# Block sums behind low parts, a late product ahead of a turn, and a filler after each lone dilated score

## The chip, the cores and the metric

The kernel runs on one core of a Trainium2 chip. The metric is the device time of one execution in microseconds (us); the time of a kernel is the median of its runs.

## The reference

A decoder trunk of two layers on 1024 tokens of width 1024, in float32. Each layer normalises its input, makes one wide projection of it, runs two kinds of attention on the parts, gates and merges them, and ends with a convolutional feed-forward network of inner width 2816:

```python
for l in range(DEPTH):                       # DEPTH = 2
    h = rmsnorm(x, norm1[l])
    proj = h @ w_in[l]
    qa, ka, va, qb, kb, vb, gate_pre = jnp.split(proj, splits, axis=-1)
    o_a = dilated_mixture(...)               # windows 128, 512, 2048 at dilations 1, 4, 16; softmax with a slope
    o_b = stick_breaking_attention(...)      # sigmoid(z) times the running product of 1 - sigmoid(z)
    gates = jax.nn.sigmoid(gate_pre + b_gate[l])
    merged = g_a * (o_a @ w_br[l, :OUT_A]) + g_b * (o_b @ w_br[l, OUT_A:])
    x = x + merged @ w_o[l]
    h2 = rmsnorm(x, norm2[l])
    up = h2 @ w_up[l]
    x = x + (gelu(conv(up[:, :D_FF])) * up[:, D_FF:]) @ w_down[l]
return rmsnorm(x, norm_f)
```

## The kernel before

**Products in two parts.** Every float32 operand is split into a high part and a low part (`split`, L130: a cast on ScalarE, L131, and the rest by a subtraction on VectorE, L132), and every product is three matmuls on TensorE: high by high, high by low, low by high. Names with `hi` or `h` at the end (w_hi, t_hi, hh, p0h) are high parts, those with `lo` or `l` (w_lo, t_lo, hl, p0l) are low parts. A weight piece comes by DMA into w_raw or in_a, and ScalarE and VectorE make w_hi and w_lo of it.

**Attention with dense work between.** In the first half of each layer TensorE's order is written by hand. `attend` (L325) goes through 36 items: 16 of stick-breaking attention (B00 to B17), 4 near ones of the dilated mixture with dilation 1 (N00 to N11), and 16 far ones (T00 to T17). An item has scores (L603, L604: z from keys and queries), turns (transposes of the probabilities: L659 for B, L730 for N, L834 to L836 for T) and products of the turned probabilities with the values (L670 for B, L742 for N, L844 and L846 for T). A turn is followed by `parts` (L606), which makes the high and low part of the turned probabilities. The product of one turn comes after the next turn, and the last product of an item, `late`, is carried over into the next item, where it stands behind the first turn. Between all these steps stands dense work, the projections: `dense.advance(rate)` adds the rate of the phase to a sum and emits one step, six matmuls of 128x512, whenever the sum passes 1. It also calls `aside`, which emits one step of side work. `dense.step()` emits a step of dense work alone. The dense steps up to N11 are plain products (L168 to L170); after it come the seven-products (L918 to L920).

**Seven-products and block sums.** The gates, far keys, queries and values are multiplied as two-by-two blocks with seven block products in place of eight. For this, sums of the blocks of the normalised input are needed: S[3], S[1], S[2] and S[4], each of four pieces of 128x512. `block_sums` (L924) plans them as side work: S[3] after B14 and B17, S[1] from the scores of N01 on, S[2] from those of N11 on, S[4] after that. A step `first` (L941 to L943) makes a piece of a sum by three operations on GpSimd, `further` (L950, L951) makes a later sum from the one before by two on VectorE, all in the tile h_sum, and `in_two` splits a piece into t_hi and t_lo (S[4] into the places of hh and hl). The products of a pair (`pair_rest`, `run`) take S[2] first (into the bank i_a, which L1064 then adds to u), then S[1] (into i_c, L1069), then S[3] (into i_a again, L1077), h itself, and S[4]. Ahead of them GpSimd makes sums of the weight blocks in four operations (L1044, L1047, L1050, L1051).

**Who orders what.** TensorE takes its instructions as they are written. On VectorE, ScalarE, GpSimd and the DMA queue of SyncE a scheduler sets the order when the program is built; `tc.high_priority` raises some instructions, among them those of `parts`, and `tc.issue_after(x)` keeps instructions behind x in the order of their engine.

Of the kernel before, what the change touches and what calls it, by code (L numbers as in the profile page):

```python
# [11 lines left out]
ALU = mybir.AluOpType  # L12
# [4 lines left out]
T = 1024  # L17
# [30 lines left out]
def f32(ap):  # L48
    return ap.bitcast(F32)
# [3 lines left out]
def trunk_kernel(ctx, tc, x, norm1, w_in, b_gate, w_br, w_o, norm2, w_up, conv_w, conv_b, w_down, norm_f, out, depth=None, probe=None):  # L53
# [75 lines left out]

    def split(hi, lo, src, eng=None):  # L130
        act.copy(hi, src)  # L131
        (eng or dve).tensor_tensor(lo, src, f32(hi), ALU.subtract)  # L132


    def weights(src, cols, place=None):
# [189 lines left out]
    def attend(dense, items):  # L325

        late = None
        for i, (name, first, rest, rate, make) in enumerate(items):  # L330
            if i == 0:
                dense.until(first)
                dense.step()
                dense.step()
                sc, micro = make()
                for f in sc:
                    f()
                    dense.advance(rate)
                dense.done.add(name + "s")
            dense.until(rest)  # L340
            seq = []
            for m, (t, p) in enumerate(micro):
                seq.append(t)
                if m == 0 and late:
                    seq.append(late)
                if m >= 1:
                    seq.append(micro[m - 1][1])

            def late(f=micro[-1][1], name=name):
                f()  # L350
# [12 lines left out]
            if pending or i + 1 == len(items):  # L363
                seq.append(late)
                late = None
            gap = max(1.0, len(seq) * 0.7 / max(1, len(nxt)))
            at = 0.0
            for j, f in enumerate(seq):
                if nxt and j >= at:
                    nxt.pop(0)()  # L370
                    at += gap
                    if not nxt:
                        dense.done.add(items[i + 1][0] + "s")
                    dense.advance(rate)
                f()
                dense.advance(rate)
            if pending:
                dense.until(pending[1])
                dense.step()
                dense.step()  # L380
                begin()
            if nxt:
                for f in nxt:
                    f()
                    dense.advance(rate)
                dense.done.add(items[i + 1][0] + "s")
            micro = nmicro

# [217 lines left out]
    def parts(src, n, name):  # L606

        hi, lo = small(name + "h", F32R), small(name + "l", F32R)
        with tc.high_priority(offset=AHEAD):
            split(hi[:, :n], lo[:, :n], src[:, :n])  # L610
        return hi, lo

    def fold(dst, o):
# [310 lines left out]
    def block_sums(made):  # L924
# [5 lines left out]
        def at(t, i):  # L930
            if t == 3 and i < 2:
                if "o" not in keep:
                    keep["o"] = sb.tile([P, 2, HF], F32, tag="ot", name="h_sum2")
                return keep["o"][:, i, :]
            if "r" not in keep:
                keep["r"] = quarter("h_sum")
            return keep["r"][:, i, :]

        def first(t, a, b, i):
            r, (ah, al), (bh, bl) = at(t, i), a()[i], b()[i]  # L940
            pool.tensor_tensor(r, f32(al), f32(bl), ALU.subtract)  # L941
            pool.tensor_tensor(r, r, f32(ah), ALU.add)
            pool.tensor_tensor(r, r, f32(bh), ALU.subtract)  # L943

        def further(t, a, i):
            if t == 4:

                S[4] = half(0, 0)
            r, (ah, al) = keep["r"][:, i, :], a()[i]
            dve.tensor_tensor(r, f32(ah), r, ALU.subtract)  # L950
            dve.tensor_tensor(r, r, f32(al), ALU.add)  # L951

        def in_two(t, i):
            if t not in S:
                new_s(t)
            split(*S[t][i], at(t, i))

        b11, b12, b21, b22 = (lambda n=n, k=k: half(n, k) for k in range(2) for n in (1, 0))
        todo = []
# [19 lines left out]
        if made is None:  # L979
            plan({"B14"}, {0: [third(0)], 6: [third(1)]})  # L980
        plan({"B17"}, {0: [third(2)], 1: [cast(0)], 4: [cast(1)], 6: [third(3)], 9: [cast(2)], 14: [cast(3)]})
        series({"N01s"}, 1, lambda i: first(1, b12, b11, i), 7, 6)
        series({"N11s"}, 2, lambda i: further(2, b22, i), 1, 1)
        series({"plain", "01", "v0"}, 4, lambda i: further(4, b21, i), 1, 1)
        return todo

# [931 lines left out]
```

## Time and profile before

| | |
|---|---|
| median of 3 runs | 2699.85 us (2698.91 to 2700.82) |
| the profiled execution | 2700.87 us, its span 2699.1 us |
| mean granted clock of TensorE | 0.996 of full speed |
| busy: TensorE (PE), VectorE (DVE), ScalarE (ACT), GpSimd (POOL) | 2653.6, 2107.1, 1313.9, 742.1 us |

In the rows of a timeline the first number is the start in us from the start of the span, the second the time from start to end (of all, where x2 or more stand at the end), then the engine, the line, the operation, output and inputs, and the shape. In brackets stands how long the engine was idle before it, and which instruction ended the idleness. In the rows of waits the three numbers are the us in total, the number of waits and the longest of them. Matmuls overlap, so the distance between two starts says more than a duration. Layer 1 repeats the pattern of layer 0 some 1340 us later.

### The profile page before, as it was taken

Reading aid. Unit: us, or ns where it says so; the run is one execution under the profiler, and the core shown is the slowest. Engines: PE = TensorE matmul, PEld = TensorE weight load, DVE = VectorE, ACT = ScalarE, POOL = GpSimd, SP = SyncE. Lnnn points to the kernel's source line nnn. Section 1 sums busy time; section 2 is a strip of 40 time slices with the busy share of each in tenths; the row PEclk is TensorE's granted clock in tenths of the full one; section 3 lists DMA queues with packets and bytes.
Section 4 is the critical chain, followed back from the end, with each engine's and each line's share of the span. In section 5 each row is a group of like instructions: output and inputs, shape, how many; then the busy total and the mean of one; then the engine's idle time right before and its main releaser. Section 6 shows DMA issues by size and latency. Waiting matters only on the chain. (4 is left out here: it accounts for less than half of the span.)

```text
span 2699.1 us, 37164 instructions
## 1 busy us (share of the span) xinstructions
PE 2653.6 (98%) x13098; PEld 2228.6 (83%) x13098; DVE 2107.1 (78%) x3168; ACT 1313.9 (49%) x2434; POOL 742.1 (27%) x533
## 2 busy tenths in 40 slices
PE   8999999999999999999999999999999999999999
PEld 8877888888888888888889878888888888888888
DVE  5888866675789988897658887666858888988865
ACT  5656544364455555432335665434635555454225
POOL 2004133222233434321120042332211443343210
PEclk9999999999999999999999999999999999999999
DMA  4133489763234444688401334988732443447863
GB/s 153 32 99 120 132 242 236 203 230 117 82 119 170 143 153 147 220 323 320 161 32 47 101 116 145 254 213 223 237 88 77 155 157 138 167 145 256 334 242 122
DMA packets 399559, 448.88 MB, mean 166 GB/s; under 512 B 22044, under 2 KB 319372, under 8 KB 397836
## 3 DMA queue, kind: packets, MB, share of 16 engines
q1 hardware_dynamic: 399372, 446.49, 51.9%
q8 instruction: 104, 1.70, 0.3%
q14 instruction: 83, 0.68, 0.1%
HBM read 300.61 MB, written 142.67 MB: 164 GB/s over the span
## 5 line engine op out<-in xcount | busy, mean ns | idle before, releaser
L132 DVE TENSOR_TENSOR w_lo<-up_a,w_hi 128x512 fp32r<-128x512 f32 x240 | 237.5, 996 | 20.1 <-ACT w_hi L131 20.1
L131 ACT CAST w_hi<-up_a 128x512 fp32r<-128x512 f32 x240 | 149.4, 623 | 184.0 <-PE u_a L919 45.3
L1666 DVE TENSOR_TENSOR x<-x,d_ps 128x512 f32<-128x512 f32 (+1 forms) x228 | 152.1, 671 | 78.5 <-PE d_ps L1660 77.7
L1397 POOL TENSOR_TENSOR cv<-cv 128x512 f32<-128x512 f32 x88 | 132.3, 1515 | 248.8 <-DVE cv L1392 126.3
L132 DVE TENSOR_TENSOR w_lo<-w_raw,w_hi 128x512 fp32r<-128x512 f32 x172 | 130.8, 763 | 62.0 <-ACT w_hi L131 59.4
L131 ACT CAST w_hi<-w_raw 128x512 fp32r<-128x512 f32 x172 | 106.7, 621 | 129.6 <-PE o_ps L169 63.4
L131 ACT CAST w_hi<-in_a 128x512 fp32r<-128x512 f32 x140 | 86.7, 620 | 150.6 <-PE i_a L919 84.3
L132 DVE TENSOR_TENSOR g<-cv,g 128x512 fp32r<-128x512 f32 x154 | 152.5, 991 | 5.2 <-ACT g L131 2.7
L1658 PE MATMUL d_ps<-gd_in,w_hi 128*128 128x512 f32 (+1 forms) x340 | 130.3, 383 | 1.1 <-ACT w_hi L131 0.5
L1660 PE MATMUL d_ps<-gd_in,w_lo 128*128 128x512 f32 (+1 forms) x340 | 129.7, 382 | 0.0
L1659 PE MATMUL d_ps<-gd_in,w_hi 128*128 128x512 f32 (+1 forms) x340 | 129.7, 382 | 0.0
L918 PE MATMUL u_a<-hh,w_hi 128*128 128x512 f32 x320 | 124.7, 390 | 0.3 <-DVE u L1548 0.2
L919 PE MATMUL u_a<-t_lo,w_hi 128*128 128x512 f32 x320 | 124.5, 389 | 0.0
L918 PE MATMUL u_a<-t_hi,w_hi 128*128 128x512 f32 x320 | 124.5, 389 | 0.0
L920 PE MATMUL u_a<-hh,w_lo 128*128 128x512 f32 x320 | 124.5, 389 | 0.0
L919 PE MATMUL u_a<-hl,w_hi 128*128 128x512 f32 x320 | 124.5, 389 | 0.0
L920 PE MATMUL u_a<-t_hi,w_lo 128*128 128x512 f32 x320 | 124.5, 389 | 0.0
L132 DVE TENSOR_TENSOR w_lo<-in_a,w_hi 128x512 fp32r<-128x512 f32 x140 | 112.5, 803 | 3.7 <-ACT w_hi L131 3.3
L1051 POOL TENSOR_TENSOR in_a<-in_a 128x512 f32<-128x512 f32 x28 | 38.0, 1358 | 281.3 <-DVE w_lo L132 281.3
L131 ACT CAST g<-cv 128x512 fp32r<-128x512 f32 x154 | 94.9, 616 | 41.7 <-POOL cv L1397 30.1
L1658 PE MATMUL d_ps<-gd_in,wd 128*128 128x512 f32 (+1 forms) x292 | 113.9, 390 | 0.0
L1660 PE MATMUL d_ps<-gd_in,wd 128*128 128x512 f32 (+1 forms) x292 | 112.8, 386 | 0.0
(398 smaller groups left out, 8716.5 us busy)
## 6 DMA issues: line engine op xcount, KB each, us to landing
gd<-g SPq DMA_DIRECT2D x154, 512.0 KB, 3.7
gd_in<-gd SPq DMA_DIRECT2D x154, 512.0 KB, 6.0
up_a<-in_w_up_dram SPq DMA_DIRECT2D x80, 512.0 KB, 4.9
in_a<-in_w_in_dram SPq DMA_DIRECT2D x56, 512.0 KB, 6.5
w_raw<-in_w_in_dram SPq DMA_DIRECT2D x100, 256.0 KB, 3.0
t_kq<-tk SPq DMA_DIRECT2D x64, 384.0 KB, 8.2
wd_raw<-in_w_down_dram SPq DMA_DIRECT2D x22, 1024.0 KB, 9.4
gin<-gs SPq DMA_DIRECT2D x32, 512.0 KB, 4.0
```

Of the source, the lines that this page charges most:

```text
L131: act.copy(hi, src)
L132: (eng or dve).tensor_tensor(lo, src, f32(hi), ALU.subtract)
L918: pe.matmul(o, w[0][:, c], rh, start=(first and i == 0), stop=False, skip_group_check=True)
L919: pe.matmul(o, w[0][:, c], rl, start=False, stop=False, skip_group_check=True)
L920: pe.matmul(o, w[1][:, c], rh, start=False, stop=(last and i == 3), skip_group_check=True)
L1051: pool.tensor_tensor(a11, a22, a11, ALU.subtract)
L1397: return lambda: pool.tensor_tensor(dst, a, b, ALU.subtract)
L1658: pe.matmul(o[:, sub], wh[:, c], gh[:, sub], start=(i == 0 and k in (0, 4, 5)), stop=False, skip_group_check=True)
L1659: pe.matmul(o[:, sub], wh[:, c], gl[:, sub], start=False, stop=False, skip_group_check=True)
L1660: pe.matmul(o[:, sub], wl[:, c], gh[:, sub], start=False, stop=(i == m - 1), skip_group_check=True)
L1666: dve.tensor_tensor(x, x, o[:, sub], ALU.add)
```

## The change

It has three parts.

- **Block sums.** `parts` notes the low part that it emitted last, and the two operations of `further` and the split of `in_two` are issued behind it in VectorE's order (`behind`). No wait is added, only an order. The plans of S[1] and S[2], which ran one after the other from N01s and from N11s, become one from N01s: for each piece i, `first` at step 6i, its split 7 steps later, `further` one step after that and the split two steps after that.
- **The late product.** For i == 1 (item B01) it stands ahead of the first turn and not behind it.
- **Lone scores.** Where an item's scores stand without turns between them and the item is a far one, each score is followed by `dense.step()`: always one block of six matmuls, no side step, and nothing added to the sum of rates.

The program has the same instructions before and after, in number and kind.

```diff
+    def behind():
+        return tc.issue_after(mark["low"]) if "low" in mark else contextlib.nullcontext()
...
                 if m == 0 and late:
-                    seq.append(late)
+                    seq.insert(0 if i == 1 else 1, late)
...
                 for f in nxt:
                     f()
-                    dense.advance(rate)
+                    if items[i + 1][0][0] == "T":
+                        dense.step()
+                    else:
+                        dense.advance(rate)
...
         with tc.high_priority(offset=AHEAD):
-            split(hi[:, :n], lo[:, :n], src[:, :n])
+            mark["low"] = split(hi[:, :n], lo[:, :n], src[:, :n]).ins
...
             r, (ah, al) = keep["r"][:, i, :], a()[i]
-            dve.tensor_tensor(r, f32(ah), r, ALU.subtract)
-            dve.tensor_tensor(r, r, f32(al), ALU.add)
+            with behind():
+                dve.tensor_tensor(r, f32(ah), r, ALU.subtract)
+                dve.tensor_tensor(r, r, f32(al), ALU.add)
...
-            split(*S[t][i], at(t, i))
+            with behind():
+                split(*S[t][i], at(t, i))
...
-        series({"N01s"}, 1, lambda i: first(1, b12, b11, i), 7, 6)
-        series({"N11s"}, 2, lambda i: further(2, b22, i), 1, 1)
+        steps = {}
+        for i in range(4):
+            for k, f in (
+                (0, lambda i=i: first(1, b12, b11, i)),
+                (7, lambda i=i: in_two(1, i)),
+                (8, lambda i=i: further(2, b22, i)),
+                (10, lambda i=i: in_two(2, i)),
+            ):
+                steps.setdefault(6 * i + k, []).append(f)
+        plan({"N01s"}, steps)
         series({"plain", "01", "v0"}, 4, lambda i: further(4, b21, i), 1, 1)
```

Lines of the changed kernel are a few higher: L134 is the subtraction of `split` (L132 before), L959 and L960 the two operations of `further`, L1082 the addition to u (L1064), L926 to L928 the seven-products, L611 and L612 the scores.

**VectorE near item N01**, layer 0: p0l_2899 and p0l_2930 are low parts of its turned probabilities, t_lo and h_sum belong to the block sums, w_lo to weights of the plain products, ql and on to other steps of attention. Before:

```order
L132 TENSOR_TENSOR t_lo_3097<-h_sum_2729,t_hi_3096 128x512 x2
L132 TENSOR_TENSOR p0l_2899<-t0_2896,p0h_2898 128x128
L132 TENSOR_TENSOR w_lo_2941<-w_raw_2938,w_hi_2940 128x512
L132 TENSOR_TENSOR t_lo_3097<-h_sum_2729,t_hi_3096 128x512 x2
L950 TENSOR_TENSOR h_sum_2729<-hh0_108,h_sum_2729 128x512 x2
L132 TENSOR_TENSOR w_lo_2947<-w_raw_2944,w_hi_2946 128x512
L951 TENSOR_TENSOR h_sum_2729<-h_sum_2729,hl0_109 128x512
L132 TENSOR_TENSOR p0l_2930<-t0_2924,p0h_2929 128x512
L619 TENSOR_TENSOR on_2496<-o0_2883,fold_2935 64x512
```

And now:

```order
L134 TENSOR_TENSOR w_lo_2941<-w_raw_2938,w_hi_2940 128x512
L134 TENSOR_TENSOR p0l_2899<-t0_2896,p0h_2898 128x128
L134 TENSOR_TENSOR w_lo_2947<-w_raw_2944,w_hi_2946 128x512
L134 TENSOR_TENSOR p0l_2930<-t0_2924,p0h_2929 128x512
L564 SCALAR_TENSOR_TENSOR ql_2794<-q_ps_2876,qt_2793 64x512
L627 TENSOR_TENSOR on_2496<-o0_2883,fold_2935 64x512
L134 TENSOR_TENSOR p0l_2964<-t0_2959,p0h_2963 128x384
L565 SCALAR_TENSOR_TENSOR ql_2794<-q_ps_2876,qt_2793 64x512
L134 TENSOR_TENSOR t_lo_2749<-h_sum_2729,t_hi_2748 128x512
```

The t_lo and h_sum that stood ahead of the two low parts have gone further back; only w_lo_2941 and w_lo_2947 are left there.

**VectorE near item N11**, some 60 us later: i_a_3549 is the bank that the first seven-product of a pair fills with S[2], and L1064 (L1082) takes it out. The last rows ahead of it before:

```order
L132 TENSOR_TENSOR w_lo_3520<-in_a_3425,w_hi_3519 128x512
L132 TENSOR_TENSOR p0l_3485<-t0_3480,p0h_3484 128x384
L1018 TENSOR_TENSOR rf_3429<-q1s_3428,r_ps_3468 128x512
L951 TENSOR_TENSOR h_sum_2729<-h_sum_2729,hl1_332 128x512
L950 TENSOR_TENSOR h_sum_2729<-hh1_331,h_sum_2729 128x512
L132 TENSOR_TENSOR w_lo_3573<-in_a_3425,w_hi_3572 128x512
L132 TENSOR_TENSOR hl0_109<-h_sum_2729,hh0_108 128x512
L132 TENSOR_TENSOR p0l_3562<-t0_3557,p0h_3561 128x384
L951 TENSOR_TENSOR h_sum_2729<-h_sum_2729,hl1_332 128x512
L1064 TENSOR_TENSOR u_3517<-u_3517,i_a_3549 128x512
```

And now:

```order
L134 TENSOR_TENSOR p0l_3562<-t0_3557,p0h_3561 128x384
L134 TENSOR_TENSOR hl0_109<-h_sum_2729,hh0_108 128x512
L960 TENSOR_TENSOR h_sum_2729<-h_sum_2729,hl1_332 128x512
L959 TENSOR_TENSOR h_sum_2729<-hh1_331,h_sum_2729 128x512
L627 TENSOR_TENSOR on_2496<-o0_3516,fold_3581 64x512
L134 TENSOR_TENSOR hl0_109<-h_sum_2729,hh0_108 128x512
L960 TENSOR_TENSOR h_sum_2729<-h_sum_2729,hl1_332 128x512
L134 TENSOR_TENSOR p0l_3596<-t0_3590,p0h_3595 128x512
L959 TENSOR_TENSOR h_sum_2729<-hh1_331,h_sum_2729 128x512
L134 TENSOR_TENSOR hl0_109<-h_sum_2729,hh0_108 128x512
L960 TENSOR_TENSOR h_sum_2729<-h_sum_2729,hl1_332 128x512
L1082 TENSOR_TENSOR u_3523<-u_3523,i_a_3549 128x512
```

From p0l_3442 (its name is p0l_3462 now) to L1064 stood 13 instructions; now 22 stand between, among them t_lo_3200, the last low part of S[2], as the ninth. The sums h_sum with hh1 and the splits into hl0_109 are S[4]'s. They stood on both sides of L1064 and now stand ahead of it but for one.

**TensorE at the far items T02 and T03**, whose scores are z_4457, z_4458 and z_4472 (z_4481 now), with i_c_4437 a bank of the seven-products. Before:

```order
L603 MATMUL z11_4458<-t_kq_4268 128x256
L604 MATMUL z11_4458<-t_kq_4268 128x256
L603 MATMUL z10_4472<-t_kq_4300 128x128
L604 MATMUL z10_4472<-t_kq_4300 128x128
L603 MATMUL z10_4472<-t_kq_4300 128x128
```

And now:

```order
L611 MATMUL z11_4458<-t_kq_4268 128x256
L612 MATMUL z11_4458<-t_kq_4268 128x256
L926 MATMUL i_c_4437<-t_hi_3096,w_hi_4394 128x512
L927 MATMUL i_c_4437<-t_lo_3097,w_hi_4394 128x512
L928 MATMUL i_c_4437<-t_hi_3096,w_lo_4395 128x512
L926 MATMUL i_c_4437<-t_hi_3096,w_hi_4394 128x512
L927 MATMUL i_c_4437<-t_lo_3097,w_hi_4394 128x512
L928 MATMUL i_c_4437<-t_hi_3096,w_lo_4395 128x512
L611 MATMUL z10_4481<-t_kq_4292 128x128
```

Six matmuls of dense work stand between the scores of two items that stood next to each other.

More of the change, by code (lines that the diff above doesn't have):

```diff
@@ L1 @@
+import contextlib
 import concourse.bass as bass
@@ L131, in split @@
         act.copy(hi, src)
-        (eng or dve).tensor_tensor(lo, src, f32(hi), ALU.subtract)
+        return (eng or dve).tensor_tensor(lo, src, f32(hi), ALU.subtract)
+    def behind():
+        return tc.issue_after(mark["low"]) if "low" in mark else contextlib.nullcontext()
     def weights(src, cols, place=None):
```

## The prediction

> **What bounds the kernel now.** I read the page's busy table first, then TensorE's waits summed over the span, and then the timelines of the engines at each place that the change touches.
>
> ```profile
> PE 2653.6 (98%) x13098; PEld 2228.6 (83%) x13098; DVE 2107.1 (78%) x3168; ACT 1313.9 (49%) x2434; POOL 742.1 (27%) x533
> PE o L742 <- DVE p0l L132: 10.6, 8, 3.1
> PE z L603 <- DVE st L826: 2.9, 2, 1.5
> PE sb_t L659 <- DVE beta L649: 2.6, 2, 1.3
> PE o L844 <- DVE p1l L132: 1.8, 3, 0.7
> ```
>
> TensorE is busy 98% of the span. It issues the same matmuls after the change, so only its idle time (2699.1 less 2653.6, 45.5 us) and its clock can be won, while any engine that comes late adds time. Three of the waits have the change's names in them. The largest is for low parts of near probabilities (p0l, made by VectorE at L132): 10.6 us in 8 waits. With two layers that is four waits in each, and the timeline of layer 0 has them at 264.04, 270.71, 326.46 and 330.30 (1.28, 3.07, 0.71 and 0.24 us, 5.30 in all, half of 10.6). So I work in layer 0's times and take each sum twice. The second wait is for score banks in the dilated phase (two waits, 2.9 us), the third for stick weights (two waits, 2.6 us).
>
> **Place 1, near item N01.** First TensorE, then VectorE, then ScalarE:
>
> ```profile
> 264.04 0.33 PE L742 MATMUL o<-p0l,v 128*128 128x128 f32 x1 [1.28 <-DVE p0l L132]
> 270.71 0.39 PE L742 MATMUL o<-p0l,v 128*128 128x256 f32 x1 [3.07 <-DVE p0l L132]
> 272.18 0.63 PE L170 MATMUL r_ps<-hh,w_lo 128*128 128x512 f32 x1
> ```
> ```profile
> 261.23 2.44 DVE L132 TENSOR_TENSOR t_lo<-h_sum,t_hi 128x512 fp32r<-128x512 f32 x2
> 263.70 0.29 DVE L132 TENSOR_TENSOR p0l<-t,p0h 128x128 fp32r<-128x128 f32 x1
> 263.90 1.45 DVE L132 TENSOR_TENSOR w_lo<-w_raw,w_hi 128x512 fp32r<-128x512 f32 x1
> 265.28 2.37 DVE L132 TENSOR_TENSOR t_lo<-h_sum,t_hi 128x512 fp32r<-128x512 f32 x2
> 269.98 0.68 DVE L132 TENSOR_TENSOR p0l<-t,p0h 128x512 fp32r<-128x512 f32 x1
> ```
> ```profile
> 262.12 0.27 ACT L131 CAST p0h<-t 128x128 fp32r<-128x128 f32 x1
> 262.28 1.14 ACT L131 CAST w_hi<-w_raw 128x512 fp32r<-128x512 f32 x2
> 263.81 0.57 ACT L131 CAST p0h<-t 128x512 fp32r<-128x512 f32 x1
> ```
>
> VectorE took the low part at 263.70 and the next at 269.98. The high parts that they need were ready at 262.12 + 0.27 = 262.39 and 263.81 + 0.57 = 264.38. What stood ahead was t_lo twice (2.44 us), then w_lo, t_lo twice, three steps h_sum and w_lo again: the block sums. In the changed order only one w_lo stands ahead of each low part. First low part: VectorE is free at 261.23, one w_lo takes until 261.8 alone or 262.7 at the 1.45 of 263.90, the high part is there at 262.39, and a low part of 128 columns takes 0.2, so it is ready by 262.6 to 262.9. TensorE wants it at 264.04 - 1.28 = 262.76. Second: its high part is there at 264.38, the w_lo ahead of it has its w_hi by 262.28 + 1.14 = 263.42 and ends by 264.9, and the low part is ready by 265.5. TensorE wants it at 270.71 - 3.07 - 1.28 = 266.36. Both waits go: **-4.35 us a layer, -8.7 in all**.
>
> Behind the second wait a matmul of 512 columns takes 0.63 us (272.18), where others take 0.39 (1611.03). That is a stretch at half clock; behind the wait of the next place stands another, which shows its size:
>
> ```profile
> 421.21 0.63 PE L918 MATMUL i_c<-t_hi,w_hi 128*128 128x512 f32 x1
> 421.64 0.63 PE L919 MATMUL i_c<-t_lo,w_hi 128*128 128x512 f32 x1
> 424.72 0.39 PE L919 MATMUL i_c<-t_lo,w_hi 128*128 128x512 f32 x1
> 424.95 0.40 PE L920 MATMUL i_c<-t_hi,w_lo 128*128 128x512 f32 x1
> 1610.34 0.39 PE L742 MATMUL o<-p0l,v 128*128 128x256 f32 x1 [3.06 <-DVE p0l L132]
> 1611.03 0.39 PE L169 MATMUL r_ps<-hl,w_hi 128*128 128x512 f32 x1
> 1759.61 0.63 PE L918 MATMUL i_c<-t_hi,w_hi 128*128 128x512 f32 x1
> ```
>
> From 421.21 matmuls start 0.43 us apart, from 424.72 on 0.23 apart. So the stretch lasts some 3.4 us and costs 3.4 x (1 - 0.23/0.43) = 1.6. In layer 1 the wait of 3.06 at 1610.34 has none behind it (1611.03 takes 0.39), while the shorter one of place 2 has one in both layers (421.21 and 1759.61). So a wait of 1.5 to 3 us brings the half clock at some phases and not at others. Here layer 0 gains **-1.6**.
>
> [...]
>
> **Place 2, lone dilated scores (T03).** T03's scores stand right behind T02's and wait for their banks from 417.85 (419.31 less 1.46):
>
> ```profile
> 419.31 0.33 PE L603 MATMUL z<-t_kq 128*128 128x128 f32 x1 [1.46 <-DVE st L826]
> 417.40 1.51 DVE L132 TENSOR_TENSOR w_lo<-in_a,w_hi 128x512 fp32r<-128x512 f32 x1 [0.18 <-ACT w_hi L131]
> ```
>
> The bank comes free when VectorE has read the scores before, which it does behind a w_lo of 1.51 us. After the change six dense matmuls stand there: 6 x 0.23 = 1.4 us, so T03 starts at the same 419.3, but with 1.4 us of TensorE's work done. Their operands are parts of an earlier weight piece than that w_lo. The filler is drawn forward, not added: one block less stands behind the last join, where the branch products follow and I see no wait that six matmuls would cover. Gain **-2.8** over two layers. With it go the two half clocks behind it, **-3.2** more. The t_kq transfers that follow depend on the same scores and move along. Elsewhere in this phase a filler only changes places with a turn or a product. The waits for low parts there (o L844, 1.8 us in three) I take as unchanged; the bounds are -1.8, if they go, and as much above.
>
> **Place 3, the turn of stick item B01.**
>
> ```profile
> 78.39 0.44 PE L659 MATMUL sb_t<-ident,beta 128*128 128x128 f32 x2 [1.30 <-DVE beta L649]
> 78.58 0.36 PE L670 MATMUL sb_o<-sbh,vb 128*128 128x256 f32 x1
> 79.08 0.45 PE L168 MATMUL k_ps<-hh,w_hi 128*128 128x512 f32 x1
> 73.83 0.55 DVE L132 TENSOR_TENSOR sbl<-sb_t,sbh 128x384 fp32r<-128x384 f32 x1
> ```
>
> TensorE waits 1.30 us for stick weights and then runs the late product (78.58 to 79.08, 0.50 us). That product now runs inside the wait: its low part was ready at 73.83 + 0.55. The wait stays 0.8. I take 0.45 of the 0.50: **-0.9** in two layers, 0 to -1.0.
>
> **Place 4, near item N11, where the work goes.** The block sums that left N01 still have to be made, and the sums S[2] have a due time: the first seven-product takes them. TensorE, VectorE, GpSimd:
>
> ```profile
> 314.40 0.60 PE L730 MATMUL t<-ident,p 128*128 128x128 f32 x4
> 322.68 0.39 PE L919 MATMUL i_a<-t_lo,w_hi 128*128 128x512 f32 x1
> 328.32 0.48 PE L918 MATMUL i_a<-t_hi,w_hi 128*128 128x512 f32 x1
> ```
> ```profile
> 314.87 3.49 DVE L951 TENSOR_TENSOR h_sum<-h_sum,hl 128x512 f32<-128x512 f32 x2
> 322.39 0.54 DVE L132 TENSOR_TENSOR p0l<-t,p0h 128x384 fp32r<-128x384 f32 x1
> 322.86 0.67 DVE L1018 TENSOR_TENSOR rf<-q1s,r_ps 128x512 f32<-128x512 f32 x1
> 326.93 0.67 DVE L1064 TENSOR_TENSOR u<-u,i_a 128x512 f32<-128x512 f32 x1
> ```
> ```profile
> 312.18 2.21 POOL L1051 TENSOR_TENSOR in_a<-in_a 128x512 f32<-128x512 f32 x1 [45.68 <-DVE w_lo L132]
> 314.35 1.74 POOL L1044 TENSOR_TENSOR in_a<-in_a 128x512 f32<-128x512 f32 x1
> 316.17 1.63 POOL L1047 TENSOR_TENSOR in_a<-in_a 128x512 f32<-128x512 f32 x1
> 317.88 1.63 POOL L1050 TENSOR_TENSOR in_a<-in_a 128x512 f32<-128x512 f32 x1
> ```
>
> Before, VectorE reached L1064 (u<-u,i_a) at 326.93 and ended at 327.60, 0.7 ahead of 328.32, where TensorE writes that bank again. In the changed order 22 instructions stand between the low part p0l_3462 and L1082 (the same statement), S[4]'s sums among them, which nobody needs yet. Twenty are 128x512 at 0.60 from start to start, two 128x384 at 0.47 (322.39 to 322.86): 12.9 us, with L1082 13.6. The low part can't start before its high part: transposes at 314.40 and 0.60 long, a cast of 0.57 as at 263.81, so 315.8. It ends at 316.4, and L1082 at 330.0 with no hindrance. But GpSimd runs until 319.5, and beside it two L951 took 3.49 us where 0.60 + 0.68 = 1.28 would do: 1.1 more for each. I take two such hits, as that row has them, and L1082 ends at 332.2.
>
> The wait for S[2]'s last low part (ninth of the 22, 8 x 0.60 + 0.47 = 5.3) comes first: 316.4 + 5.3 + 2.2 = 323.9, wanted at 322.68: **+1.2**. Then L1082 is wanted at 328.32 - 0.71 + 1.2 = 328.8: **+3.4**. The old waits of 0.71 and 0.24 go, as their low parts now stand ahead. Together +3.65 a layer, **+7.3** in two. Without hits it is 330.0 against 327.6, less 0.95: +1.4 a layer; with a third hit +4.75. A wait of 3.4 us is as long as the one at 270.71, so I also charge a half-clock stretch in each layer: **+3.2** (0 to 3.2). Behind L1082 stand a w_lo, S[4]'s low part and L1087, all in time for a TensorE that is itself 3.6 later.
>
> [...]
>
> **Sum.** -8.7 - 1.6 - 2.8 - 3.2 - 0.9 + 7.3 + 3.2 = -6.7 us on the profiled execution's own 2700.87 us (span 2699.1 and 1.8 around it): 2694.2. That execution is 1.0 above the median of 2699.85, so against the runs I predict **2693.1 us**.
>
> **Rivals.**
> - B, a light N11: no hits, no half clock there. Gains 17.2, cost 2.8: -14.4, so 2685.5. For it: which of VectorE's instructions meets which product is a matter of tenths. Against it: the L951 row.
> - C, slower: VectorE is held for the whole of GpSimd's four products, 2.21 + 1.74 + 1.63 + 1.63 = 7.2 us instead of 2.2. The two waits grow from 1.2 and 3.4 to 6.2 and 3.4, and a second half clock follows: 5.0 + 1.6 more a layer, 13.2 in two, so 2706.3. It turns slower from a loss of 4 to 5.5 us on, with and without the second half clock (6.7 / 2 = 3.35 above 2.2). Against it: before, the L951 pair lost 2.2 beside the same products.
> - D, the half clock doesn't follow waits: three stretches stay, none comes: -8.7 - 2.8 - 0.9 + 7.3 = -5.1, so 2694.8.
> - E, the change doesn't do what it says: the w_lo ahead of the second low part waits for its weights, so that only the first wait shrinks. Two waits of 3.07 and the half clock come back: +7.7, so 2700.8. Against it: both w_hi casts were done by 263.42.
>
> **How the numbers follow.** My forecast 0.50, B 0.20, C 0.12, D 0.10, E 0.08. About 0.2%, 5.4 us, is what a measurement of this kernel can tell from no change, so faster means below 2694.5. The forecast's own spread (+-1.1 from a third hit or one fewer, +-1.6 for one half clock) puts 0.35 of its 0.50 below that; with B that is 0.55. Same: 0.15 + D + E = 0.33. Slower: C, 0.12. The range takes in B and E and reaches 2703, leaving out most of C.
>
> **What would show it.** In the changed profile: no wait of o<-p0l over 0.3 us near 258 to 266; VectorE's h_sum and t_lo behind the p0l there. Six i_c matmuls between two groups of scores near 412, and no half clock behind. A new row in TensorE's waits, i_a<-L1082 of some 3 us twice, and i_a<-t_lo of some 1 us twice. If L1082 comes in time, B holds and I was too high; if the two rows come to over 8 us a layer, C. I would be wrong altogether if a new wait of some us appears in the dilated phase, whose order I take as harmless.

## The result: 0.2% slower, and the profile after

The changed kernel takes 2705.21 us (median of 19 runs, 2701.57 to 2709.77), the kernel before 2700.12 us in 19 runs beside it: ratio 1.0020, 95% interval 1.0014 to 1.0026, so 5.1 us slower. I had predicted 2693.1 us and a range of 2685 to 2703: the sign was wrong, and the time lies outside the range. The profiled execution after took 2708.21 us with a span of 2706.4, 7.3 above the span of before.

I first look at the page's busy table and at TensorE's waits summed over the span (us in total, number, longest):

```profile
PE 2657.5 (98%) x13098; PEld 2229.0 (82%) x13098; DVE 2106.2 (78%) x3168; ACT 1313.2 (49%) x2434; POOL 739.1 (27%) x533
```
```profile
PE i_a L926 <- DVE u L1082: 7.1, 2, 3.5
PE r_ps L173 <- DVE ql L565: 6.5, 4, 1.9
PE sb_t L667 <- DVE beta L657: 1.7, 2, 0.9
PE i_a L927 <- DVE t_lo L134: 1.7, 2, 0.9
```

The wait for low parts, 10.6 us in 8 before, has left the head of the list. In its place stand two others. One was forecast: i_a for u at L1082, 7.1 us. The other was not: **r_ps for ql at L565**, 6.5 us in four waits, where the same pair had 2.7 us in two before (r_ps L168 for ql L557); the two new ones are at N01. TensorE's busy time is 2657.5 us, 3.9 more for the same matmuls. The granted clock of the whole span is 0.996 in both, so I leave that difference unexplained.

Where the clock fell is read from the same stretches of 20 us in both kernels. The columns are the stretch, its length, the busy time of TensorE, of its weight loads, of VectorE, ScalarE and GpSimd (each with instructions), then the granted clock, the DMA share and GB/s. Before, near N01, N11, T03 and the N01 of layer 1:

```profile
262.00:282.00 20.00, 15.65 (x77) 12.71 (x76) 18.75 (x27) 8.66 (x18) 4.34 (x3) 0.91 0.33 101
320.00:340.00 20.00, 19.04 (x98) 15.62 (x97) 18.58 (x32) 9.10 (x19) 5.36 (x4) 1.00 0.30 91
411.00:431.00 20.00, 18.55 (x92) 15.40 (x91) 13.72 (x26) 8.33 (x18) 6.25 (x4) 0.91 1.12 274
1604.00:1624.00 20.00, 16.94 (x89) 13.93 (x88) 18.24 (x28) 7.98 (x16) 2.05 (x2) 1.00 0.42 132
```

And after:

```profile
262.00:282.00 20.00, 17.42 (x84) 13.98 (x83) 11.84 (x19) 9.59 (x19) 9.87 (x8) 0.91 0.40 118
320.00:340.00 20.00, 15.59 (x73) 12.50 (x72) 16.90 (x28) 7.84 (x15) 2.55 (x2) 0.91 0.23 67
411.00:431.00 20.00, 19.48 (x106) 16.20 (x105) 16.11 (x28) 10.11 (x22) 5.84 (x4) 1.00 1.06 261
1604.00:1624.00 20.00, 17.34 (x82) 13.90 (x81) 12.38 (x20) 10.10 (x20) 9.47 (x7) 0.91 0.39 118
```

A clock of 0.91 over 20 us is one half-clock stretch: 0.09 x 20, some 1.8 us of clock lost (over the 3.41 us from 268.97 in the profile after, the clock is 0.50). T03 has lost its stretch, as forecast. N11 has one, as forecast. But N01 kept its own in layer 0, and got one in layer 1, where none was.

For the sum by place I take the start times of matmuls of the same number in the program's order, and compare how long each place takes from its first to its last, both layers together. All kernels have the same 13098 matmuls. The filler changes their order, so the bounds are matmuls ahead of which every kernel has done the same ones. T, the far items with the last join, goes from 390 to 567 us in layer 0 of before; the branch products (br_ps) behind it are taken from there to 600:

| place | predicted, us | profile after less before, us |
|---|---|---|
| N01 (waits -8.7, half clock -1.6) | -10.3 | **-2.3** (-1.85 and -0.45) |
| T, the far items (-2.8, -3.2) | -6.0 | -6.0 (-2.80 and -3.23) |
| branch products | 0 | **+3.2** (+0.53 and +2.67) |
| B01 | -0.9 | -0.9 (-0.44 and -0.45) |
| N11 (waits +7.3, half clocks +3.2) | +10.5 | +10.0 (+5.03 and +4.95) |
| everywhere else | 0 | +3.3 |
| sum | -6.7 | +7.3 |

"Everywhere else" holds -0.1 to +3.4 us in the twelve kernels below, and most of it stays open. One piece can be named, the waits of u_a for u at L1566 in the second half of a layer: 1.7 us here and 0.2 before. They are 1.4 to 3.8 us in all kernels with the late product and in e7, and 0.2 to 0.6 in the others; what makes them is not shown. The runs' 5.1 us lie between the five places' +4.0 and the profile's +7.3. So two terms failed: N01 by 8.0 us, and the branch products behind the last join, which the sum had at nothing, by 3.2. The 1.8 us of clock per stretch compare with the 1.6 that I had charged.

**N01 after.** TensorE in layer 0, then VectorE:

```profile
265.76 0.39 PE L750 MATMUL o<-p0h,v 128*128 128x256 f32 x1 [0.36 <-ACT p0h L133]
266.48 0.39 PE L750 MATMUL o<-p0l,v 128*128 128x256 f32 x1 [0.34 <-DVE p0l L134]
268.98 0.76 PE L173 MATMUL r_ps<-hh,w_hi 128*128 128x512 f32 x1 [1.87 <-DVE ql L565]
269.54 0.63 PE L174 MATMUL r_ps<-hl,w_hi 128*128 128x512 f32 x1
```
```profile
264.78 0.69 DVE L134 TENSOR_TENSOR w_lo<-w_raw,w_hi 128x512 fp32r<-128x512 f32 x1 [3.40 <-ACT w_hi L133]
265.74 0.69 DVE L134 TENSOR_TENSOR p0l<-t,p0h 128x512 fp32r<-128x512 f32 x1 [0.27 <-ACT p0h L133]
266.35 0.68 DVE L564 SCALAR_TENSOR_TENSOR ql<-q_ps,qt 64x512 fp32r<-64x512 f32 x1
266.96 0.68 DVE L627 TENSOR_TENSOR on<-o,fold 64x512 f32<-64x512 f32 x1
267.56 0.54 DVE L134 TENSOR_TENSOR p0l<-t,p0h 128x384 fp32r<-128x384 f32 x1
268.13 0.69 DVE L565 SCALAR_TENSOR_TENSOR ql<-q_ps,qt 64x512 fp32r<-64x512 f32 x1
```

The second low part starts at 265.74 and is ready at 266.43, 0.9 us later than I had it, since the w_lo ahead of it waits 3.40 us for its w_hi. Even so the waits for high and low parts are down to 0.36 and 0.34 us. But the product that follows them at once, r_ps at 268.98, writes a bank that VectorE must have read first: q_ps, which ql at L565 takes out from 268.13 to 268.82. It stands behind the p0l of 265.74, the first ql, on and another p0l. So 4.35 us of waits became 0.36 + 0.34 + 1.87 = 2.57, and the r_ps behind it starts 0.56 us apart from its next (268.98, 269.54) at a duration of 0.63: half clock. Before, the r_ps behind the second low part started at 271.33, ahead of its ql at L557 (272.35), so it had another bank then; why the changed program gives it this one is not shown.

**N11 after**, TensorE, then VectorE:

```profile
321.66 0.50 PE L927 MATMUL i_a<-t_lo,w_hi 128*128 128x512 f32 x1 [0.87 <-DVE t_lo L134]
330.18 0.61 PE L926 MATMUL i_a<-t_hi,w_hi 128*128 128x512 f32 x1 [3.55 <-DVE u L1082]
330.59 0.63 PE L927 MATMUL i_a<-t_lo,w_hi 128*128 128x512 f32 x1
```
```profile
314.56 1.28 DVE L134 TENSOR_TENSOR t_lo<-h_sum,t_hi 128x512 fp32r<-128x512 f32 x1
315.77 1.77 DVE L134 TENSOR_TENSOR w_lo<-in_a,w_hi 128x512 fp32r<-128x512 f32 x1
320.93 0.68 DVE L134 TENSOR_TENSOR t_lo<-h_sum,t_hi 128x512 fp32r<-128x512 f32 x1
329.44 0.68 DVE L1082 TENSOR_TENSOR u<-u,i_a 128x512 f32<-128x512 f32 x1
```

Forecast were 1.2 us for t_lo, 3.4 for L1082 and a half clock; there are 0.87, 3.55 and a half clock. The two hits by GpSimd are there as well: t_lo takes 1.28 and w_lo 1.77 beside its products of 1.30 (314.00) and 1.62 us (315.38), where 0.68 is usual, 1.7 us together (I had 2.2).

**The end of the far items and the branch products.** Two rows of TensorE before and one after, all of layer 0:

```profile
554.25 0.39 PE L844 MATMUL o<-p1l,t_v 128*128 128x256 f32 x1 [0.75 <-DVE p1l L132]
575.50 0.50 PE L168 MATMUL br_ps<-oh_b,br_w 128*128 128x512 f32 x1 [0.28 <-DVE gin L1309]
```
```profile
576.21 0.50 PE L173 MATMUL br_ps<-oh_b,br_w 128*128 128x512 f32 x1 [0.79 <-DVE gin L1327]
```

The wait for a low part at the end of the far items is gone: between 505 and 567 us of before the changed kernel gains 1.9 us in this layer. Behind the last join six matmuls fewer are left, and TensorE waits 0.79 us in place of 0.28 for gin, the step in which VectorE takes an earlier branch product out of its bank. The first of these steps begins at 574.76 before and at 575.47 after, so VectorE is no earlier there. All waits of br_ps for gin come to 2.7 us, 0.8 before.

### The profile page after: what moved, and what is told of

The parts are those of the page before. It is cut to its first block, busy times and chain, and to the rows that moved or that the text cites. A ratio compares the mean times of both kernels' runs of the same rounds, so it can differ in the third digit from the quotient of the medians.

```text
span 2706.4 us, 37158 instructions
## 1 busy us (share of the span) xinstructions
PE 2657.5 (98%) x13098; PEld 2229.0 (82%) x13098; DVE 2106.2 (78%) x3168; ACT 1313.2 (49%) x2434; POOL 739.1 (27%) x533
## 5 line engine op out<-in xcount | busy, mean ns | idle before, releaser
L134 DVE TENSOR_TENSOR w_lo<-up_a,w_hi 128x512 fp32r<-128x512 f32 x240 | 236.6, 992 | 21.5 <-ACT w_hi L133 21.5
L134 DVE TENSOR_TENSOR w_lo<-w_raw,w_hi 128x512 fp32r<-128x512 f32 x172 | 129.6, 756 | 66.9 <-ACT w_hi L133 63.1
L134 DVE TENSOR_TENSOR g<-cv,g 128x512 fp32r<-128x512 f32 x154 | 152.2, 989 | 5.2 <-ACT g L133 2.8
L926 PE MATMUL u_a<-hh,w_hi 128*128 128x512 f32 x320 | 124.6, 390 | 1.7 <-DVE u L1566 1.7
L928 PE MATMUL u_a<-hh,w_lo 128*128 128x512 f32 x320 | 124.5, 389 | 0.0
L928 PE MATMUL u_a<-t_hi,w_lo 128*128 128x512 f32 x320 | 124.5, 389 | 0.0
L926 PE MATMUL u_a<-t_hi,w_hi 128*128 128x512 f32 x320 | 124.5, 389 | 0.0
L134 DVE TENSOR_TENSOR w_lo<-in_a,w_hi 128x512 fp32r<-128x512 f32 x140 | 116.6, 834 | 6.7 <-ACT w_hi L133 6.5
L1676 PE MATMUL d_ps<-gd_in,wd 128*128 128x512 f32 (+1 forms) x292 | 113.9, 390 | 0.0
L1678 PE MATMUL d_ps<-gd_in,wd 128*128 128x512 f32 (+1 forms) x292 | 112.8, 386 | 0.0
L1677 PE MATMUL d_ps<-gd_in,wd 128*128 128x512 f32 (+1 forms) x292 | 112.8, 386 | 0.0
```

The lines of the kernel that those rows point to most:

```text
L134: return (eng or dve).tensor_tensor(lo, src, f32(hi), ALU.subtract)
L926: pe.matmul(o, w[0][:, c], rh, start=(first and i == 0), stop=False, skip_group_check=True)
L928: pe.matmul(o, w[1][:, c], rh, start=False, stop=(last and i == 3), skip_group_check=True)
L1676: pe.matmul(o[:, sub], wh[:, c], gh[:, sub], start=(i == 0 and k in (0, 4, 5)), stop=False, skip_group_check=True)
L1677: pe.matmul(o[:, sub], wh[:, c], gl[:, sub], start=False, stop=False, skip_group_check=True)
L1678: pe.matmul(o[:, sub], wl[:, c], gh[:, sub], start=False, stop=(i == m - 1), skip_group_check=True)
```

## The experiments

Each expectation names its own theories. Edits are shown against the changed kernel, unless said otherwise.

**Which part loses?** Three kernels, each with one part alone. e1 has the block sums' part, e2 the late product ahead of B01's turn, e3 the filler. In e1, for example, the other two parts are undone:

```diff
-                    seq.insert(0 if i == 1 else 1, late)
+                    seq.append(late)
...
-                    if items[i + 1][0][0] == "T":
-                        dense.step()
-                    else:
-                        dense.advance(rate)
+                    dense.advance(rate)
```

> Part 1 alone (hold and merged plan of the block sums); late product and lone scores as before. Theory A, from the changed profile: what makes the change slower is part 1. Near N01 the waits fall only from 4.35 to 2.57 us a layer, with a half clock behind in both layers instead of one (-3.6 + 1.6); near N11 the two waits 0.87 + 3.55 replace 0.71 + 0.24 a layer, with two half clocks (+6.9 + 3.2). Together +8 us, about 2708. Rival B: the loss lies in the fillers drawn forward (waits behind the last join of layer 1); then part 1 alone is at most +3.

> Part 2 alone. Both theories: the two waits for stick weights fall from 1.30 to 0.86, -0.9 us in all, which may be lost in the scatter. A change of over 2 us either way would mean that the order of the late product moves something that neither theory knows.

> Part 3 alone. Theory A, as the prediction had it: the two waits before T03's scores and the two half clocks behind them go, -6.0 us; at least -2, since the changed profile still shows a wait of 0.5 and two of 0.2 in that phase. Rival B: the drawn-forward work is missed behind the last join, where the changed profile waits 2.7 us for gin in place of 0.8: then 0 to +3.

| kernel | median, us | before beside it | ratio, 95% interval |
|---|---|---|---|
| e1, block sums | 2706.92 | 2701.82 | 1.0022, 1.0013 to 1.0032 |
| e2, late product | 2701.86 | 2701.82 | 1.0003, 0.9994 to 1.0011 |
| e3, filler | 2700.86 | 2701.82 | 0.9999, 0.9990 to 1.0008 |

The block sums' part alone makes the whole loss. The filler alone gains nothing that can be measured, where I had 6 us. Its trace has the gain in the far items, -5.7 us, but it gives 3.4 back in the branch products, where br_ps waits 3.8 us for gin in place of 0.8; that is what the rival in its expectation had. VectorE of e3 shows at T03 why the wait there doesn't go as a whole:

```profile
417.07 1.57 DVE L134 TENSOR_TENSOR w_lo<-in_a,w_hi 128x512 fp32r<-128x512 f32 x1
418.56 1.77 DVE L1113 SCALAR_TENSOR_TENSOR u<-u,kq_h 128x512 fp32r<-128x512 f32 x1
420.25 1.77 DVE L134 TENSOR_TENSOR w_lo<-in_a,w_hi 128x512 fp32r<-128x512 f32 x1
```

Three VectorE steps in a row take 1.57 to 1.77 us, with GpSimd at work beside them; before, two such steps, of 1.55 and 1.51, stood ahead of the reading of the scores. TensorE works for 1.4 us more, and the bank comes free later too, so a wait is left in layer 0: 0.95 us here (422.42), 0.52 in the profile after (423.72).

**Whose steps hold L1082 up at N11?** When the first seven-product is begun, all side steps that are waiting are pressed in ahead of it, those of S[4] too, which is taken last. e4 leaves S[4]'s behind:

```diff
-                        while self.side:
+                        while self.side and "plain" not in self.side[0][0]:
```

> The changed kernel, but the steps of S[4] are no longer all emitted ahead of the first seven-product; they follow one by one behind it. Theory A: L1082 then stands ahead of most of S[4]'s steps on VectorE, so the waits of 0.87 and 3.55 a layer and the half clocks behind them go: 2705 - 8.8 - 3.2 = 2693, at least 2698. Rival: the backlog comes from S[1] and S[2] and not from S[4]; then the wait for t_lo stays, L1082 is still some us late, and the time stays within 2 us of 2705.

2698.60 us against 2701.82, ratio 0.9990 (0.9981 to 0.9999): 0.3% below the changed kernel, and N11 now takes +2.4 us instead of +10.0, both layers together. TensorE near N11:

```profile
321.11 0.50 PE L927 MATMUL i_a<-t_lo,w_hi 128*128 128x512 f32 x1 [0.25 <-DVE t_lo L134]
330.43 0.33 PE L750 MATMUL o<-p0h,v 128*128 128x128 f32 x1 [1.11 <-ACT p0h L133]
```

The wait for L1082 and its half clock are gone, that for t_lo is 0.25, and one of 1.11 for a high part is new. So 7.6 of the 10.0 us at N11 were S[4]'s steps in VectorE's queue.

**Why did N01 gain so little?** VectorE was idle for 3.40 us ahead of 264.78, waiting for a w_hi that stood on ScalarE behind a t_hi that waits for GpSimd. My first theory was that this is what keeps the second low part late. e5 takes the hold from the splits of S[3], whose t_hi that is; e6 has the edits of e4 and e5:

```diff
-            with behind():
+            with behind() if t != 3 else contextlib.nullcontext():
                 split(*S[t][i], at(t, i))
```

> The changed kernel, but the splits of S[3] are not held behind low parts (those of S[1] and S[2] and the further steps are). Theory A: near N01 the held subtraction t_lo of S[3] kept GpSimd from writing the next piece of S[1] into the same tile, ScalarE's cast t_hi of that piece stood ahead of a cast w_hi in its queue and idled 2.98 us, and with w_hi came w_lo, the second low part and ql late. Free, ScalarE casts without idling and the waits of 0.36 + 0.34 + 1.87 a layer and their half clocks go: 5.1 + 0 to 3.2 us below the changed kernel, 2697 to 2700 where that is 2705. Rival: w_raw's transfer was late by itself; then w_hi still waits and nothing is won.

> e4 and e5 in one: S[3]'s splits free, S[4]'s steps behind the first seven-product. Theory A: both places are mended and the gains add: 2690 to 2694, 5 to 8 us below e4, 0.3% below the kernel before. Rival: what the one place gains comes back as a wait elsewhere (VectorE has the same number of instructions in the same stretch); then it is no better than e4.

e5: 2705.79 against 2701.55, ratio 1.0017 (1.0008 to 1.0025). e6: 2698.98, ratio 0.9986 (0.9977 to 0.9994). So e5 gains nothing over the changed kernel, and **this theory fell**. VectorE and GpSimd of e5:

```profile
262.43 3.36 DVE L134 TENSOR_TENSOR w_lo<-w_raw,w_hi 128x512 fp32r<-128x512 f32 x2 [0.23 <-ACT w_hi L133]
265.72 0.68 DVE L134 TENSOR_TENSOR p0l<-t,p0h 128x512 fp32r<-128x512 f32 x1
268.08 0.69 DVE L565 SCALAR_TENSOR_TENSOR ql<-q_ps,qt 64x512 fp32r<-64x512 f32 x1
```
```profile
262.25 1.29 POOL L1065 TENSOR_TENSOR in_a<-in_a 128x512 f32<-128x512 f32 x1
263.63 1.62 POOL L1068 TENSOR_TENSOR in_a<-in_a 128x512 f32<-128x512 f32 x1
```

ScalarE is early now, and the two w_lo follow each other at once, but beside GpSimd's products of weight blocks they take 3.36 us instead of 1.3. The low part is where it was (265.72 for 265.74), ql is too (268.08 for 268.13), and so are the wait of 1.85 us and both half clocks. e6, with the same edit on top of e4's, can't be told from e4 (0.9990).

**Hold or plan?** e7 has the hold of steps behind low parts with the old plans of S[1] and S[2], e8 the new plan without the hold; neither has the other two parts. The edit of e7:

```diff
-        steps = {}
...
-        plan({"N01s"}, steps)
+        series({"N01s"}, 1, lambda i: first(1, b12, b11, i), 7, 6)
+        series({"N11s"}, 2, lambda i: further(2, b22, i), 1, 1)
```

> Half of part 1: the block sums' VectorE steps held behind low parts, but S[1] and S[2] planned one after the other as before. Theory A: the hold is what moves the backlog to N11; with the old plan S[2]'s steps come still later, so that the wait for its low parts grows to some 4 us a layer on top of L1082's: 2708 to 2715. Rival: the merged plan is at fault; then this one is no slower than before.

> The other half: the merged plan without the hold. Theory A: VectorE's order is nearly that of before (seven block-sum steps ahead of the second low part near N01, L1082 in time near N11), so the waits are those of before and the time is that of before within 2 us. Rival, the merged plan at fault: 2705 or more.

e7: 2720.72 against 2701.55, ratio 1.0078 (1.0066 to 1.0090). e8: 2701.15, ratio 0.9998 (0.9990 to 1.0007). The merged plan by itself does nothing that can be measured; the hold moves the work, and without the plan it costs 19 us. That is above the 2708 to 2715 us of the expectation. TensorE's waits of e7 name the steps:

```profile
PE i_a L924 <- DVE t_lo L134: 5.4, 8, 1.4
PE i_a L923 <- ACT t_hi L133: 3.5, 3, 1.7
```

With S[2] planned only from N11 on, its splits come too late for the first seven-products: 11 waits in all, and N11 takes 21.4 us longer.

**Is it ql?** My next theory: what ends N01 is ql, and low parts that are early don't help as long as ql stands behind them. e9 ranks the two ql steps ahead:

```diff
+        with tc.high_priority(offset=AHEAD):
             dve.scalar_tensor_tensor(la[0:64], o[0:64], scale, f32(qa[0:64]), ALU.mult, ALU.subtract)
             dve.scalar_tensor_tensor(lb[64:128], o[64:128], scale, f32(qb[64:128]), ALU.mult, ALU.subtract)
```

> The changed kernel, with the two VectorE steps that make ql in queries_half ranked ahead of the low parts of probabilities that are ready beside them; nothing else differs. Theory 1 (near N01 the last of the three waits is for ql L565, which stands on VectorE behind on and the second low part): r_ps<-ql goes from 1.87 to about 0.8 us in both layers, the two half-clock stretches at 269.0 and 1610.5 may go with it (1.6 us each), and the ratio to before falls from 1.002 to between 1.0005 and 1.0015. Theory 2 (VectorE is full there, what is put ahead only pushes the second low part back): r_ps<-ql shrinks but a wait for p0l of 0.5 to 1 us takes its place, and the ratio stays at 1.002.

> The kernel with both amendments (fourth sums' steps not pressed in ahead of the first seven-product, third sums' splits not held), and ql ahead as well. Theory 1: the amended kernel's 0.9986 of before falls by a further 1 to 3 us, to 0.9975 to 0.998. Theory 2: it stays at 0.9986.

e9: 2703.47 against 2700.59, ratio 1.0010 (1.0001 to 1.0019), as theory 1 had it; the interval overlaps that of the changed kernel, so the traces have to show the gain. e10, with the edits of e4, e5 and e9: 2694.54, ratio **0.9970** (0.9959 to 0.9982), 6.0 us faster than before and 4 us below e6, which ran on another occasion. Theory 1 had 0.9975 to 0.998, which the interval takes in. In e10 no stretch at half clock is left near N01, N11 or T. TensorE and VectorE of e9 near N01:

```profile
266.67 0.39 PE L751 MATMUL o<-p0l,v 128*128 128x256 f32 x1 [0.34 <-DVE p0l L134]
268.08 0.47 PE L173 MATMUL r_ps<-hh,w_hi 128*128 128x512 f32 x1 [0.79 <-DVE ql L566]
268.39 0.39 PE L174 MATMUL r_ps<-hl,w_hi 128*128 128x512 f32 x1
```
```profile
267.24 0.69 DVE L566 SCALAR_TENSOR_TENSOR ql<-q_ps,qt 64x512 fp32r<-64x512 f32 x1
268.57 0.54 DVE L134 TENSOR_TENSOR p0l<-t,p0h 128x384 fp32r<-128x384 f32 x1
```

The second ql goes from 268.13 to 267.24, the wait from 1.87 to 0.79, and the low part that now stands behind it (268.57) keeps nobody waiting. The next matmuls take 0.39: the half clock is gone, in layer 1 as well. N01 takes 6.3 us less than before in e9 and 7.1 less in e10, where it was 2.3 less in the changed kernel. The clock of e10 near N01 and N11:

```profile
262.00:282.00 20.00, 18.64 (x95) 15.24 (x95) 15.41 (x22) 10.09 (x20) 3.20 (x3) 1.00 0.43 134
320.00:340.00 20.00, 18.57 (x94) 14.80 (x93) 18.88 (x31) 8.34 (x18) 5.20 (x4) 1.00 0.33 93
```

**What is the filler worth once the rest is mended?** e11 is e6 without the filler, e12 the changed kernel without the block sums' part, so with the late product and the filler.

```diff
-                    if items[i + 1][0][0] == "T":
-                        dense.step()
-                    else:
-                        dense.advance(rate)
+                    dense.advance(rate)
```

> The kernel with both amendments, without the filler step behind lone dilated scores. By the prediction's sum for that place (6 us for waits and half clocks) this is 6 us slower than the amended kernel: 1.0008 of before. By what the filler alone gave (0.9999 of before) it is the same as the amended kernel: 0.9986 to 0.999.

> Late products in front of a turn and the filler step, without the block sums' part. If the parts add up: 1.0003 times 0.9999 of before, so no difference (0.9995 to 1.0008), and the whole loss of the changed kernel stands with the block sums' part. If the parts help each other (the prediction's 6 us in T plus 0.9 near B01): 0.9975.

e11: 2700.40 against 2700.59, ratio 0.9998 (0.9989 to 1.0007), so 0.0012 or some 3 us above e6, which ran on another occasion; the intervals overlap, so this is an indication and not proof. e12: 2698.81, ratio 0.9993 (0.9984 to 1.0002): 1.9 us less than before by the ratio, which the interval can't tell from nothing.

The traces show the same places in all kernels, as us more or less than before, both layers together. There is one profile of each:

| kernel | N01 | N11 | T | branch products | B01 |
|---|---|---|---|---|---|
| changed kernel | -2.3 | +10.0 | -6.0 | +3.2 | -0.9 |
| e1 block sums | -2.3 | +10.0 | -3.7 | -0.2 | 0.0 |
| e2 late product | 0.0 | 0.0 | -0.8 | +0.8 | -0.9 |
| e3 filler | +1.1 | 0.0 | -5.7 | +3.4 | 0.0 |
| e4 S[4] late | -2.5 | +2.4 | -6.7 | +1.0 | -0.9 |
| e5 S[3] free | -1.9 | +10.0 | -4.1 | +0.5 | -0.9 |
| e6 e4 and e5 | -1.9 | +2.3 | -4.5 | +1.8 | -0.9 |
| e7 hold, old plan | -2.4 | +21.4 | -0.2 | +0.2 | 0.0 |
| e8 plan, no hold | -1.5 | 0.0 | +0.8 | -0.2 | 0.0 |
| e9 ql ahead | -6.3 | +10.8 | -4.7 | +1.0 | -0.9 |
| e10 e6 and ql ahead | -7.1 | +2.1 | -6.3 | +1.2 | -0.9 |
| e11 e6, no filler | -1.8 | +2.0 | +1.3 | +0.2 | -0.9 |
| e12 late and filler | 0.0 | 0.0 | -5.1 | +2.5 | -0.9 |

N11 goes by the hold and by where S[4] stands, N01 by the hold and by where ql stands, B01 by the late product. At N01 the kernels without the hold scatter from -1.5 to +1.1, where a half clock came in 4 of their 10 passages (last section). T and the branch products go by the filler. T is -4.1 to -6.7 with it in eight kernels and -3.7 to +1.3 without it in six (before at 0 among them), the means are -5.4 and -0.4. The branch products are at +0.5 to +3.4 with it and at -0.2 to +0.8 without it, the means are +1.8 and +0.1. In layer 0 the first wait of br_ps for gin is 0.69 to 1.06 us in all eight and at most 0.28 in the six.

## Why the prediction was wrong

**Place 1 is the step that failed**: "Both waits go -4.35 us a layer, -8.7 in all", and with them a half clock. The waits for low parts did go but for 0.34 us, with 0.36 for a high part beside it. What I didn't ask is what TensorE meets next, once they come. It is a bank that ql must free, and that ql stands four rows behind the second low part in the changed order that I had printed. From the trace of before the wait could not be seen, since r_ps had another bank there. From the changed program it could, with the bank of each product looked up beside that order: three steps of about 0.6 us stand between the low part and ql at L565, so with the low part ready by 265.5 (begun at 264.9) ql ends 0.6 x 4 + 0.7 = 3.1 us after that start, at 268.0. In the same sum TensorE, which wanted the low part at 266.36, goes on at once and is at r_ps some 0.6 us later (266.48 to 267.11 in the profile after): a wait of about 1 us a layer, which I left out. It became 1.87, as the low part itself began 0.8 us later. So the gain in waits was 1.8 us a layer and not 4.35. That ql sets this end is shown by e9, where only ql moves.

The half clock at N01 was the second half of the same step: -1.6 forecast, +1.6 found. Waits of 2.57 us in all, spread over three places, still brought it in this profile, and in both layers. In the five kernels without the hold, waits of equal length at N01 brought a stretch in 4 of 10 passages (last section), so both numbers stand for single executions.

**Place 2**, "Gain -2.8 over two layers" and -3.2 for half clocks: the -6.0 is what the far items gave, but in part by luck, and the step that failed is another one, behind the last join. At T03 the mechanism was right: the six matmuls do stand in the wait, 1.46 became 0.52 in layer 0 and none in layer 1, and no kernel with the filler has a half clock there. Up to 505 us of layer 0 and the same place of layer 1 the changed kernel has -2.9 of the -6.0, since between 388 and 410 us it falls 1.0 us behind, 0.44 of it in new small waits. The other -3.1 comes at the end of the far items, in part from waits for low parts (row 554.25), which I had taken as unchanged. What failed is "I see no wait that six matmuls would cover" behind the last join, a term put at nothing: the branch products wait for VectorE, and the place costs 3.2 us in the profile after. By the means above the filler gains 5.0 us in T and gives 1.7 back in the branch products, 3.3 net; the runs have 0 to 3 (e3 against before, e6 against e11).

**Place 3** held in its place: the stick weights are waited for 0.86 instead of 1.30, and the trace of e2 shows -0.9 us for it alone, too little for the runs to tell (1.0003). **Place 4** held as a sum and nearly in each term; e4 shows that most of the backlog is S[4]'s.

**The rivals.** E put the danger at the right place, a second wait at N01 that stays, and gave it 0.08; and its reason came true too, a w_lo that waits 3.40 us for its w_hi. But that is not what decides: e5 frees ScalarE and nothing is gained. D, that half clocks don't follow waits, fell: with ql ahead and nothing else (e9) both stretches at N01 go, and its waits fill at most 44% of a window, where no window at N01 with up to 54% brought one (last section). C did not happen, the hits at N11 cost 1.7 us and not 7.2. No rival had a new wait on a bank at N01 or a wait in the branch products. These two make the wrong sign: 8.0 and 3.2 of the 11.8 us between the forecast's -6.7 and the median's +5.1.

## What to carry to other kernels

When a wait is removed, walk on along the waiting engine to the next instruction that needs something, and look up in the changed order of the other engines where its releaser stands; the gain ends at that instruction, whatever the first wait was. Work drawn forward into a wait is missing where it stood: ask what it covered there. A hold that keeps work off one place moves the work to the next due time: steps that nobody needs there yet have to be kept out of that queue (S[4] here, 7.6 us), or they bring back more than was saved. Here the changed order also came with another bank for r_ps, so each step that reads and frees a bank needs its rank reviewed when another is put ahead of it.

## What the runs showed of the hardware

**Half clock and idle time at N01.** In each profile the stretches at half clock start at whole multiples of 3.413 us from one another (268.97, 330.41, 1364.65, 1610.41 and 1671.85 in the profile after, which is 0, 18, 321, 393 and 411 times 3.413 behind the first). So the span can be cut into windows of that length. At N01, a window at half clock came behind each of the 18 windows in which TensorE was idle for 57% or more, and behind none in the ten passages whose idlest window had at most 54% (14 profiles, two layers). In e3 the stretch went on for a second window, behind one that was itself at half clock and 31% idle. The two cases next to the limit, e2 and e11, each with the window behind; the first busy time, of 3.41 us, is TensorE's, and the clock is the third number from the end:

```profile
268.39:271.80 3.41, 1.57 (x8) 1.40 (x9) 3.41 (x6) 1.10 (x2) 0.00 (x0) 1.00 0.44 133
271.80:275.21 3.41, 3.41 (x20) 2.85 (x20) 3.31 (x7) 1.69 (x3) 0.00 (x0) 1.00 0.34 109
```
```profile
266.57:269.98 3.41, 1.46 (x7) 1.16 (x8) 3.08 (x6) 1.10 (x2) 0.00 (x0) 1.00 0.60 173
269.98:273.39 3.41, 3.41 (x11) 2.70 (x10) 0.56 (x1) 0.48 (x1) 0.00 (x0) 0.50 0.46 141
```

So at N01 the idle share of one window tells the cases apart, and the longest wait does not: waits of 0.36, 0.34 and 1.87 us left the window ahead of 268.97 idle for 70% in the profile after, and a stretch came; in layer 1 of before the wait of 3.06 us that ended at 1610.34 fell across two windows, idle for 50% and 40%, and none came. In the seven kernels with the hold and ql behind, the waits at N01 (0.58 to 0.89 us and, some 0.6 us of work later, 1.84 to 1.88) brought a stretch in 14 of 14 cases. In the five kernels without the hold, 1.28 us, some 3.6 us of work and then 3.06 to 3.08 brought one in 4 of 10. What differs among the ten is where the windows lay. Slid over all places, the waits of before idle away over 56% of some window at 78% of the places, those of the profile after at 45 to 48%, both estimates from these two traces. With 4 of 10 and 14 of 14 found, the windows did not lie evenly over these places; what sets where they lie is not shown. With 0.60 to 0.79 and then 0.77 to 0.79 (e9, e10) it is at most 44% of a window at any place, and none came in 4. The 57% are not a limit for other places: at T03 a stretch followed 43% in before and none followed 43% in e1, and the one at 1364.65 in the profile after followed 27%.

**VectorE beside GpSimd.** A VectorE step on 128x512 took 0.68 us alone (320.93 in the profile after), and 1.57 to 1.77 with GpSimd at work beside it (e3); two in a row took 3.36 beside GpSimd's products of 1.29 and 1.62 (e5). So freeing ScalarE at N01 was worth nothing: VectorE lost there what it had gained, and the low part came at 265.72 for 265.74. In ten such steps (N11 in the profile after, T03 in before, after and e3) the end came 0.54 to 0.56 us behind the end of the GpSimd product beside it: in e3 at 418.64 behind 418.08, 420.33 behind 419.78 and 422.02 behind 421.48, in the profile after at 419.92 behind 419.37, 421.62 behind 421.07 and 423.33 behind 422.78. These ten steps took 1.12 to 1.78 us, and in each the end went with that of the product. Not every step is hit: in the profile after u<-u,i_a took 0.69 at 418.20, beside a GpSimd product that ran from 418.07 for 1.30, and w_lo 0.69 at 264.78, beside one that ran from 264.89 for 1.70; what sets these apart is not shown.
